# A decoder layer in split fp32 on one core: another order of the same instructions on all engines

## The chip, the cores and the metric

The kernel runs on one core of a Trainium2 chip. The core has a matmul engine (TensorE, PE in the profile; PEld is its loading of weights), three engines for elementwise work (VectorE or DVE, ScalarE or ACT, GpSimd or POOL) and SyncE (SP), from whose queue most DMA transfers are issued; some are issued from POOL's queue. Each engine works through its own queue strictly in order; semaphores hold an instruction until what it reads is written and what it overwrites has been read. The metric is the device time of one execution in microseconds (us); lower is better.

## The reference

One post-norm decoder layer over 512 tokens of width 1024, all in float32. What is computed, cut to its lines:

```python
h = x @ w_in[l]
y_a = nsa_attention(nsa_q, cmp_k, cmp_v, slc_k, slc_v, win_k, win_v, nsa_gate, ...) @ w_nsa_out[l]
y_b = gated_deltanet(gdn_qkv, gdn_beta, gdn_decay, gdn_gate, ...) @ w_gdn_out[l]
mix = (jax.nn.sigmoid(gate_a) * y_a + jax.nn.sigmoid(gate_b) * y_b) @ w_o[l]
x = layer_norm(DEEPNORM_ALPHA * x + mix, ln1_g[l], ln1_b[l])
f = conv_ffn(x, ffn_w_up[l], ffn_conv_w[l], ffn_w_down[l])
x = layer_norm(DEEPNORM_ALPHA * x + f, ln2_g[l], ln2_b[l])
```

The attention (8 heads of 64, 2 key groups) has three branches: keys compressed in blocks of 32, selected blocks of 64, and a window; each is a softmax with distance penalties, and the branches are added with sigmoid gates. The gated DeltaNet (4 heads of 128) passes q, k and v through a causal convolution of 4 taps and silu, solves a triangular system in each chunk of 64 tokens, and carries a state from chunk to chunk. The feed-forward part has a width of 2816, with a causal convolution of 3 taps behind the up-projection and a gated product.

## The kernel before

Every large matrix product is done in three passes so that it keeps float32 accuracy. An operand is split into a high part (rounded to the fast matmul type fp32r) and the residue, and `product` adds three matmuls per 128 rows of the contraction:

```python
PE.matmul(ps, wh[k], mh_(k), ...)   # L532, high x high
PE.matmul(ps, wh[k], ml_(k), ...)   # L534, high x residue of the activations
PE.matmul(ps, wl[k], mh_(k), ...)   # L535, residue of the weights x high
```

A weight tile comes by DMA into `raw` (L511, on SP's queue, 512 KB, three buffers). `split_w` then makes, for each half, `wh` by a cast (L518 on ACT, or L520 on DVE or POOL) and `wl` by a subtraction (L522, on DVE or POOL), three buffers each. The products of the input projection collect in PSUM tiles called gps (two banks in turn), so a new product can begin only when the one before the last has been read out.

The first 460 us or so interleave, on all engines, the input projection with what hangs on it. The names that the change and the prediction speak of are these.

- `conv_silu` makes the convolution of q, k and v: acc (L681 on ACT, then L689 on DVE, or a tap by L686 on ACT and L687 on POOL), then th (L692, ACT) and the result (L699 on DVE: vraw for v). `trans4` transposes vraw on PE (L703, into dps).
- `queries` reads one gps three times: q on ACT (L962) and DVE (L963), then qf on ACT (L964). `keys` does the same for kh (L948, ACT) and kl (L950, DVE).
- `scores` makes scores with two matmuls (L1079, L1080, into aps), a masked maximum on DVE (L1083), exponentials on ACT (L1085), and a scaling by one over the sum (L1087, then L1094 on ACT or L1096 on DVE). `flip` transposes them on PE (L1112), splits them (L1115, L1116), and multiplies by the values (L1126, L1132). At a head's end ob (L1134, ACT) and oT (L1138, DVE) take the result out.
- `gdn_inv` solves the triangular system by steps of tmp and xs on DVE (L815, L816) and small matmuls (L831 to L871).
- `merge` gates the two mixers' projections (mt, L1158 on ACT, L1236 and L1238 on DVE).
- `sums` and `sums_o` (L561, L551) are DMA transfers on POOL's queue between DRAM regions. They form sums of weight blocks, wsum (2816 KB each) and osum (1024 KB each), that later stages load as weights in place of some products.

From about 460 us on, the feed-forward part runs: up-projection (pu), convolution and gate, then the down-projection (px, pz). The last normalization ends the program.

The order of the work isn't left to the order in which the code is written. At the end, `queues(tc)` takes the instructions of each engine as they were made, numbered from 0, and strings them into the order that the table QUEUES names; TURNS then interleaves the five queues into one sequence:

```python
chain(rows[k])                      # one engine's instructions in the order of QUEUES
chain([next(names[x]) for x, n in re.findall(r"([A-Z])(\d*)", TURNS) for _ in range(int(n or 1))])
```

In TURNS "DP4A" means the next instruction of DVE, four of PE, one of ACT (G is POOL, S is SP). The semaphores are placed for that sequence, and buffers change hands along it.

Of the kernel before, what the change touches and what calls it, by code (L numbers as in the profile page):

```python
# [71 lines left out]
def layout(a):  # L72
# [60 lines left out]
    "PE": """0-9 14 11-12 17 10 13 15 18 16 19-20 23 29-30 26 24 21-22 31 27 25 32 41 35 28 38 42-43 39 33 36 40 50 53 37 34 54 47  # L133
44 51-52 55 45 62 65 48-49 59 63 46 64 60 56 61 74 66 75 71 76 57 72 67 86 58 77 68-69 73 87 70 83 78-80 88 84 89 85
95-96 90 81 107 82 108 92-93 98 109-110 94 111 91 112 99 113 97 100 114 101-103 115-148 155-178 149-152 104-105 153
106 154 183-205 207 206 208-230 179-182 235-249 259 250 260-263 251 264-267 252 268 231-233 302 253-255 303 256 269
257-258 234 304-307 270-282 308 310-311 309 360-363 283-292 364-367 293-298 368 312 369-371 313 372 388-389 314 373
315 374-378 390-391 379 392-393 380-381 394-396 382 397 383 398-399 299-301 400-406 444-447 407-410 416-418 411
419-422 448-449 423-437 456-457 438-439 458 316 450 317-318 320-321 319 322 451 323 459-461 324-327 462-467 328-339
468-470 340-347 471 513-514 472 348 352 349 353 350-351 354-355 473-474 515 356-359 384-387 452 475-476 501-502  # L140
412-414 477-479 516-517 453-455 415 518-520 503 521-524 504 525-526 440-443 527-528 723 529-530 724-726 531-532 727
480-481 484 482-483 533-534 728 505 729-731 507 732 485 535 733 508 536 486-487 509-510 734-736 506 488-489 737-738
541 490 739-740 542 491-492 751-755 511 543-544 493-494 546 741-742 495 545 496 512 743 497 756-757 744 758 547
498-499 759-760 500 548-551 560-561 745-746 761-763 562 764 565-566 552 765 553 766 537-539 563-564 591 554 592 555
# [12 lines left out]
893 897 894 898-899 895 1071 1024 1203 1205-1208 900-903 1209 1204 1113-1115 1210 1219-1220 904 908-915 905-907
1211-1212 1116 1213-1214 1117 1221 1223 1215 916-923 1216 1118 1224 924-931 1222 1119-1121 1217 1225 932-935 1122-1124
960 1226 1125-1126 1227-1228 961-962 1233 1127 1218 1128-1129 963 1130 1234 1131 964-965 1132-1134 966-967 1141-1142
1135-1136 1235 968 1238 1143-1146 969-970 1147-1148 1239 1149 971 1150-1152 1240 972-973 1241 1252 1153-1154 974-975  # L160
1155-1156 1242 1236-1237 976 1243 1179 1157 1180 1158 1181 1253 1182-1185 1159 1244 1160-1164 1186 1025 1254 1187
1257-1258 1255 1137-1138 1256 1259 1139 1260 1140 1188-1194 1245 1026-1027 1261 1028 1262 1246-1247 1283 1195-1199
1248 1273 1200 1284 1201 1249 1202 1285 1274 1165-1168 1286 1250 1307 1169-1170 1308-1313 1275 1171-1173 1276 1174
1314-1315 1277 1316 1278 1175 1251 1287 1317 1176 1279 1177-1178 1263 1403-1404 1318 1264 1319 1265-1266 1280-1281
1405 1282 1406 1408 1267 1407 1409 1268 1288 1269 1289 1320-1321 1270 1322-1324 1271 1325-1326 1272 1327 1410-1412
1229 1328-1330 1422 1230-1231 1413 1290-1292 1423 1293 1232 1294-1296 1424 1414 1425-1426 1297 1427-1428 1298-1300
1379 1301 1380 1415 1302-1303 1381 1416-1418 1304 1419 1305 1382-1383 1429-1430 1306 1431 1384 1432 1443 1385 1444
1420 1445 1386-1388 1477 1447 1421 1433 1331 1446 1448 1389-1390 1434 1391 1435 1478-1479 1436 1449 1392 1437-1438
# [168 lines left out]
TURNS = """DS2PSPSPSPDSDPSPASPADPSDP2SP4SP4ASP2AD2P2ASP4APDP5DASP4APDP4DASP3APDP4DP2AP4APDP5DAP4AP3DP3DP5AP3APDP4APDP3DPDP4DSP7S  # L337
# [47 lines left out]
def queues(tc):  # L385
# [1233 lines left out]
```

## Time and profile before

| | |
|---|---|
| median of 3 runs | 817.49 us (816.06 to 818.82) |
| profiled execution: its own time | 816.13 us |
| profiled execution: span | 814.3 us |
| mean granted TensorE clock | 0.997 |
| instructions in the profile | 11,754 |
| HBM traffic | 116.72 MB read, 33.55 MB written, 185 GB/s over the span |

A row of a timeline reads: start in us, duration in us, engine, line of the kernel, operation, output<-inputs by the program's names, partitions x elements, how often in a row, and in brackets how long the engine had been idle before and which instruction ended that idle time. A row of the stages reads: the stretch and its length, then the busy us (and the number of instructions) of PE, PEld, DVE, ACT and POOL, then the granted PE clock, the busy share of the DMA engines and GB/s. Matmuls overlap in the records: a 512-wide one is listed with 0.39 us, though the next starts 0.23 us later, so a hole in PE's work is seen in the distance between starts.

### The profile page before, as it was taken

To read this page: it belongs to the slowest core of one execution; us is meant where nothing else is said; L and a number is where in the kernel's file an instruction comes from. 1 tells how busy PE (TensorE), PEld (TensorE's weight loads), DVE (VectorE), ACT (ScalarE), POOL (GpSimd) and SP (SyncE) were. 2 spreads that over 40 slices of the span, in tenths; PEclk is the share of its full clock that TensorE was granted. 3 is DMA by queue.
4 is the path that set the end of the run, shared out by engine and by line. 5 is a ranking of instruction groups with operands and counts; after the bars stand their busy time and mean duration, and the time that the engine had idled before them with its cause. 6 is when DMAs were issued, how large, how long until landed. Compare 5 with 4: busy or idle time off the path is not lost.

```text
span 814.3 us, 11754 instructions
## 1 busy us (share of the span) xinstructions
PE 800.0 (98%) x4144; PEld 670.2 (82%) x4144; DVE 595.8 (73%) x1314; ACT 409.1 (50%) x911; POOL 177.3 (22%) x172
## 2 busy tenths in 40 slices
PE   9999999999999999999999999999999999999995
PEld 8778778788888888888788898888888888888884
DVE  5667589979768964658669956576666766886997
ACT  4453578775577764413254334443443444565641
POOL 0333635042265111052200101122112011000002
PEclk9999999999999999999999999999999999999998
DMA  7326470035416912635357303698763923466763
GB/s 284 107 78 218 132 182 27 27 104 195 82 52 141 206 52 66 168 104 157 102 196 243 130 27 103 150 260 214 200 212 104 237 92 108 143 202 180 249 212 130
DMA packets 43115, 119.58 MB, mean 147 GB/s; under 512 B 3248, under 2 KB 4016, under 8 KB 42800
## 3 DMA queue, kind: packets, MB, share of 16 engines
q1 hardware_dynamic: 31280, 87.37, 33.2%
q0 software_dynamic: 11776, 31.46, 17.0%
q8 instruction: 33, 0.54, 0.3%
q14 instruction: 26, 0.21, 0.1%
HBM read 116.72 MB, written 33.55 MB: 185 GB/s over the span
## 4 chain that ended last, share of the span: by engine, by line
PE 93%; DVE 3%; ACT 1%; DMA 1%; issue 1%; SPq 0%; DVEq 0%; ACTq 0%
PE pu L532 10%; PE pu L535 10%; PE pu L534 10%; PE gps L532 8%; PE gps L535 8%; PE gps L534 8%; PE px L1488 7%; PE pz L1488 4%; PE pw L1324 3%; PE pout L1126 2%; PE aps L1112 2%; PE pu L1324 2%; PE pu L1488 2%; PE pm L532 2%; PE pm L534 2%; PE pm L535 2%
## 5 line engine op out<-in xcount | busy, mean ns | idle before, releaser
L522 DVE TENSOR_TENSOR wl<-raw,wh 128x512 fp32r<-128x512 f32 x146 | 103.9, 717 | 78.6 <-PE pu L535 34.3
L518 ACT ACTIVATE wh<-raw 128x512 fp32r<-128x512 f32 x126 | 78.9, 629 | 138.9 <-PE pu L534 94.8
L532 PE MATMUL pu<-mh,wh 128*128 128x512 f32 (+1 forms) x384 | 131.5, 373 | 0.0
L534 PE MATMUL pu<-ml,wh 128*128 128x512 f32 (+1 forms) x384 | 131.2, 373 | 0.0
L535 PE MATMUL pu<-mh,wl 128*128 128x512 f32 (+1 forms) x384 | 129.5, 373 | 0.0
L532 PE MATMUL gps<-xh,wh 128*128 128x512 f32 x320 | 124.8, 401 | 1.8 <-issue 0.9
L535 PE MATMUL gps<-xh,wl 128*128 128x512 f32 x320 | 126.4, 402 | 0.0
L534 PE MATMUL gps<-xl,wh 128*128 128x512 f32 x320 | 124.2, 399 | 0.0
L535 PEld LDWEIGHTS pu<-mh,wl 128*128 128x128 f32 x384 | 71.3, 188 | 13.1
L534 PEld LDWEIGHTS pu<-ml,wh 128*128 128x128 f32 x384 | 71.5, 188 | 12.6
L532 PEld LDWEIGHTS pu<-mh,wh 128*128 128x128 f32 x384 | 71.0, 188 | 12.7 <-ACT mh L1303 0.2
L1446 DVE SCALAR_TENSOR_TENSOR fa<-pu,fcw,fa 128x511 f32<-128x511 f32 (+1 forms) x88 | 64.7, 744 | 14.0 <-ACT fa L1443 13.4
L1452 POOL TENSOR_TENSOR fth<-fth,fa 128x512 f32<-128x512 f32 x22 | 30.3, 1382 | 199.8 <-DVE fth L1451 141.3
L532 PEld LDWEIGHTS gps<-xh,wh 128*128 128x128 f32 x320 | 60.1, 189 | 13.5 <-issue 2.6
L535 PEld LDWEIGHTS gps<-xh,wl 128*128 128x128 f32 x320 | 60.1, 189 | 10.5 <-DVE wl L522 0.2
L534 PEld LDWEIGHTS gps<-xl,wh 128*128 128x128 f32 x320 | 60.0, 188 | 10.5
L1423 ACT ACTIVATE wh<-raw 128x512 fp32r<-128x512 f32 x67 | 40.5, 627 | 37.9 <-PE px L1488 11.0
L1424 DVE TENSOR_TENSOR wl<-raw,wh 128x512 fp32r<-128x512 f32 x67 | 45.0, 694 | 14.2 <-ACT wh L1423 13.7
L522 POOL TENSOR_TENSOR wl<-raw,wh 128x512 fp32r<-128x512 f32 x30 | 39.9, 1337 | 13.9 <-ACT wh L518 7.0
L573 POOL TENSOR_TENSOR rs<-rs,minus_half 128x1 f32<-128x1 f32 x8 | 9.4, 1175 | 154.0 <-DVE rs L1282 154.0
L1085 ACT ACTIVATE sc<-sc,mn 128x384 f32<-128x384 f32 (+2 forms) x64 | 35.7, 559 | 11.9 <-DVE mn L1083 11.9
L1443 ACT ACTIVATE fa<-pu,fcw 128x512 f32<-128x512 f32 x44 | 29.8, 680 | 20.4 <-PE pu L535 18.8
(362 smaller groups left out, 1698.7 us busy)
## 6 DMA issues: line engine op xcount, KB each, us to landing
raw<-in_up SPq DMA_DIRECT2D x44, 512.0 KB, 4.2
raw<-in_wT SPq DMA_DIRECT2D x40, 512.0 KB, 3.6
wsum<-in_down POOLq DMA_DIRECT2D x6, 2816.0 KB, 21.6
raw<-wsum SPq DMA_DIRECT2D x20, 512.0 KB, 3.8
raw<-in_down SPq DMA_DIRECT2D x15, 512.0 KB, 4.0
osum<-in_wo POOLq DMA_DIRECT2D x6, 1024.0 KB, 10.0
wsum<-wsum POOLq DMA_DIRECT2D x2, 2816.0 KB, 15.6
raw<-in_wm SPq DMA_DIRECT2D x8, 512.0 KB, 3.6
```

Source lines behind the costliest of these rows:

```text
L518: A.activation(wh, r, AF.Copy)
L522: eng.tensor_tensor(wl, r, wh.bitcast(F32), op=OP.subtract)
L532: i = PE.matmul(ps, wh[k], mh_(k), start=(k == 0), stop=False)
L534: PE.matmul(ps, wh[k], ml_(k), start=False, stop=False)
L535: PE.matmul(ps, wl[k], mh_(k), start=False, stop=(k == n - 1))
L1085: A.activation(s[:, i, :n], s[:, i, :n], AF.Exp, scale=-1.0, bias=mn[:, 0, i:i + 1], accum_out=mn[:, 1, i:i + 1])
L1324: PE.matmul(ps[t], a[x](j)[:, ts], w[y][:, j % 2, :], start=fresh and j == 0 and i == 0, stop=j == TT - 1 and i == 2, skip_group_check=True)
L1423: A.activation(hi, raw[:, i], AF.Copy)
L1424: V.tensor_tensor(lo, raw[:, i], hi.bitcast(F32), op=OP.subtract)
L1446: V.scalar_tensor_tensor(acc[:, n:], ps[:, :S - n], w[:, i:i + 1], acc[:, n:], op0=OP.mult, op1=OP.add)
L1452: G.tensor_tensor(th, th, g[1], op=OP.mult)
L1488: m = PE.matmul(ps, a[x][:, j, ts], w[y], start=first and i == 0, stop=last and i == 2, skip_group_check=True)
```

## The change

Only the tables QUEUES and TURNS differ. Every engine executes the same instructions on the same tiles; some stand at other places in its queue. PE has 2,946 of its 3,886 places changed (by 2.9 places in the mean and 45 at most), DVE 886 of 1,250 (3.2, 57), ACT 510 of 798 (2.4, 19), POOL 113 of 168 (5.0, 40), SP 23 of 179 (1.9, 7). The first and the last few instructions of the program stay. Of some hundred changed lines, one pair reads:

```diff
-    "SP": """1 0 2-9 14 10 15 11 16 19 13 17-18 12 20-69 71 75-76 73-74 72 77-78 70 79-128 130-157 129 158-159 161 163 165 167-175
+    "SP": """1-2 0 3-9 14-15 12 11 10 13 16-69 71-72 75-76 74 73 77-79 70 80-128 130-156 129 157-159 161 163 165 167-172 162
```

Three places, in the order of the queues (engine operation output<-inputs, partitions x elements; the number behind a name tells one tile from another).

First, DVE near 107 us, where vraw_1158 is made, which PE then transposes. Before:

```order
L1096 TENSOR_SCALAR sc_1278<-sc_1278,mn_1279,gsig_109 128x128
L721 TENSOR_SCALAR ss0_991<-ss0_991 128x4
L520 CAST wh_1853<-raw_1847 128x512
L1083 ISA sc_1290,mn_1291<-aps_1289,cst_309 128x256
L1083 ISA mn_1291 128x1
L1096 TENSOR_SCALAR sc_1278<-sc_1278,mn_1279,gsig_109 128x128
L1083 ISA sc_1290,mn_1291<-aps_1289,cst_309 128x256
L1083 ISA mn_1291 128x1
L699 SCALAR_TENSOR_TENSOR vraw_1158<-th_1199,acc_1194 128x512
L736 SCALAR_TENSOR_TENSOR gk_1000<-rn_998,bn_325 128x4
L1087 RECIPROCAL mn_1291<-mn_1291 128x2
L734 RECIPROCAL gk_1000<-ss0_991 128x4
```

Now:

```order
L522 TENSOR_TENSOR wl_1851<-raw_1847,wh_1849 128x512
L1083 ISA sc_1290,mn_1291<-aps_1289,cst_309 128x256
L1083 ISA mn_1291 128x1
L721 TENSOR_SCALAR ss0_991<-ss0_991 128x4
L1087 RECIPROCAL mn_1279<-mn_1279 128x2
L520 CAST wh_1853<-raw_1847 128x512
L1096 TENSOR_SCALAR sc_1278<-sc_1278,mn_1279,gsig_109 128x128
L699 SCALAR_TENSOR_TENSOR vraw_1158<-th_1199,acc_1194 128x512
L736 SCALAR_TENSOR_TENSOR gk_1000<-rn_998,bn_325 128x4
L1087 RECIPROCAL mn_1291<-mn_1291 128x2
L721 TENSOR_SCALAR ss1_1059<-ss1_1059 128x4
```

The second L1096 of sc_1278 has gone behind vraw_1158 and gk_1000. The two L1083 of sc_1290 stand earlier, the first of them ahead of the weight residue wl_1851. On PE, at the same place, an L535 of gps_1857 now stands ahead of the transposes of vraw_1158.

Second, DVE near 155 us, where the scores sc_1790 are scaled (L1096), which PE then transposes. Before:

```order
L816 TENSOR_TENSOR xs_1683<-xs_1683,tmp_1685 128x4x8
L1138 TENSOR_TENSOR oT_1471<-pout_1568,ob_1622 64x512
L1083 ISA sc_1805,mn_1806<-aps_1804,cst_309 128x384
L1083 ISA mn_1806 128x1
L815 TENSOR_TENSOR tmp_1685<-lx_1666,xs_1683 128x4x7
L1087 RECIPROCAL mn_1791<-mn_1791 128x1
L816 TENSOR_TENSOR xs_1683<-xs_1683,tmp_1685 128x4x7
L1096 TENSOR_SCALAR sc_1790<-sc_1790,mn_1791,gsig_109 128x512
L815 TENSOR_TENSOR tmp_1685<-lx_1666,xs_1683 128x4x6
L1087 RECIPROCAL mn_1806<-mn_1806 128x1
```

Now:

```order
L1083 ISA sc_1805,mn_1806<-aps_1804,cst_309 128x384
L1083 ISA mn_1806 128x1
L815 TENSOR_TENSOR tmp_1685<-lx_1666,xs_1683 128x4x7
L1087 RECIPROCAL mn_1791<-mn_1791 128x1
L816 TENSOR_TENSOR xs_1683<-xs_1683,tmp_1685 128x4x7
L815 TENSOR_TENSOR tmp_1685<-lx_1666,xs_1683 128x4x6
L1096 TENSOR_SCALAR sc_1790<-sc_1790,mn_1791,gsig_109 128x512
L816 TENSOR_TENSOR xs_1683<-xs_1683,tmp_1685 128x4x6
L1087 RECIPROCAL mn_1806<-mn_1806 128x1
```

The addition oT_1471 stood ahead of the scaling; it now stands 13 instructions behind it, and one tmp_1685 of the triangular solver has moved ahead.

Third, the beginning of POOL's queue, some 30 us into the program. Before:

```order
L520 CAST wh_542<-raw_540 128x512
L522 ISA
L522 TENSOR_TENSOR wl_544<-raw_540,wh_542 128x512
L520 CAST wh_546<-raw_540 128x512
L522 TENSOR_TENSOR wl_548<-raw_540,wh_546 128x512
L687 TENSOR_TENSOR acc_507<-acc_507,tap_510 128x510
L520 CAST wh_586<-raw_584 128x512
L687 TENSOR_TENSOR acc_507<-acc_507,tap_513 128x509
L763 TENSOR_TENSOR grh_782<-cst_309,gdh_327 128x512
L520 CAST wh_590<-raw_584 128x512
```

Now:

```order
L520 CAST wh_542<-raw_540 128x512
L561 DMA wsum1_101<-in_down 1408x1x512
L522 ISA
L522 TENSOR_TENSOR wl_544<-raw_540,wh_542 128x512
L551 DMA osum1_105<-in_wo 512x1x512
L1063 MEMSET pth_332 128x2x128
L520 CAST wh_546<-raw_540 128x512
L520 CAST wh_586<-raw_584 128x512
L522 TENSOR_TENSOR wl_548<-raw_540,wh_546 128x512
L687 TENSOR_TENSOR acc_507<-acc_507,tap_510 128x510
L520 CAST wh_590<-raw_584 128x512
```

The large copy wsum1 stood at place 27 and is now the second thing that POOL does; osum1 and a MEMSET come soon behind it. The casts wh_586 and wh_590 stand further ahead among the sums acc_507.

Elsewhere: on ACT, qf_417 near 28 us stands ahead of the cast wh_478 instead of behind it; on DVE, x_896 near 94 us stands ahead of the sum acc_1102 (L689) instead of behind it, and bn_325 and one sacc_360 no longer ahead of q2_422 near 27 us; on PE, an L535 of gps_550 near 42.5 us stands ahead of the first L532 of gps_594, which needs the bank that kl_462 reads; on ACT near 167 us, an L1094 of sc_2183 stands ahead of x_1774 and ym_1781 instead of behind them. From 460 us on, some DVE subtractions wl (L522, L1424) stand behind one or two other DVE operations that they preceded.

More of the change, by code (lines that the diff above doesn't have):

```diff
@@ new lines @@
+1780 1775 1781 1776 1782-1784 1777 1785 1802 1786-1788 1803-1805 1789-1790 1814 1791 1806-1807 1815 1808 1816
+1809-1811 1817 1792 1818 1812-1813 1819-1820 1793 1821 1826 1822-1823 1794-1795 1824 1827 1825 1828-1829 1796
+1830-1831 1797-1800 1832-1833 1801 1834-1838 1850 1839-1841 1851-1852 1842 1853-1854 1843-1844 1855-1859 1845
+1860-1863 1846-1847 1874 1864 1875 1848 1876 1865-1866 1849 1877-1878 1886-1887 1879 1888 1880 1889 1867-1868 1881
+1890-1891 1882 1869 1883-1884 1892-1893 1885 1894 1870-1871 1895 1898-1900 1896 1901-1903 1897 1904-1908 1872-1873
@@ new lines @@
+3865-3866 3874 3867-3872 3881-3882 3873 3875-3876 3883 3877-3879 3884-3885""",
+    "DVE": """0-2 4 3 5-12 14 13 15-17 49-50 18 80 51 21 20 52 55 22 19 29 56 30 57 81 31 24 32 105 33 25 34-35 53 36-37 58 54 63
+38-44 94 45 92 46 64-65 59-60 73 61-62 74 71 28 47 72 82-83 75-77 84-85 66 78 67 48 70 141 26 143 142 68 144 97 99 101
+153 102-103 98 100 86-87 104 154-155 88-89 156 23 90 106-110 27 111 79 112-115 91 270 116-117 93 118-121 145-147
+122-123 69 124-128 95 129-130 157 131-132 148 133 158 134-135 159 136 162-163 137 164 138-139 161 140 165-166 96
@@ new lines @@
+1159 1176-1177 1162 1180 1165 1179 1183 1182 1140 1139 1184 1172 1185 1173 1186-1187 1192 1175 1197 1181 1178 1198
+1190 1201 1188 1202 1207-1208 1141 1189 1193 1211-1212 1191 1194 1199 1195 1203 1213-1214 1220 1204 1200 1221-1222
+1215 1209 1217 1216 1223 1219 1224 1210 1225-1228 1205 1196 1229-1230 1218 1206 1231-1235 1237 1236 1238-1240 1242
+1241 1243-1246 1248 1247 1249""",
+    "Activation": """1 0 3 2 4-5 7 6 9 8 10-13 15 14 22 19 16 25 20 23 21 26 30 27 17 24 18 28-29 32 40 33-35 41-44 36-39 45 50-52 60 46 53
@@ new lines @@
+659 665 658 669-670 652 636 672 663 667 673 677 666 660 678 671 680 674 681 675 685-686 679 688 676 668 689 693 682
+687 694 696 683 697 701 684 691 695 690 702 704-705 698 692 706 712 710-711 699 713-714 703 715 700 717 716 718
+707-708 719-720 722-723 709 726 725 728 730-731 729 732-733 721 734 727 736-737 739 724 740 742-745 738 746-747 735
+748 751 750 753 756-757 754 758 752 741 759-761 755 762 749 764-765 767-768 771 770 772 766 773 763 774-776 769
+777-797""",
+    "Pool": """8 137 9 101 1 10 12 11 3 13 0 4-6 14-16 18-21 7 103 25-26 31 22 24 2 34 33 100 32 27 37 104 28-29 35 30 41 38 17 23 42
@@ L382 @@
+P3S2P2DP3AP4DAP3DP3DSPAP3AP3DP2DP4DPAP2SPDP2AP3DPAP2AD2SP4APDP2APDP3DPAPDPSP2DP2AP3DAP3ADSP3DASP4APDP3DP3DP5DPAP3SDPA
+P2DPAP2DP2DPAP2DPSP2D2P3SPAPDP3DAPDP2DP2APDSP2DPDGPAP2DP3D2PAP2DP2DPSP2D2PSAGP2APSDP2DP3DPSP2D2P2AP2AP2DPAP2D2AP4DP3DS
+P2APDSPAPDP3DP3DP2DP3ADP2APDP3DP3DPDP3SP2DP4DP3DPD2PGP3DP3DP3DP5SDP4SP2DSD6GD3S2"""
 PINS = """"""
```

466 lines of the change are left out of this document (221 added, 245 removed).

## The prediction

> **What bounds the kernel now.** I read the busy times and the chain first, then the busy time by stage, then the matmul engine's (PE's) own waits.
>
> ```profile
> PE 800.0 (98%) x4144; PEld 670.2 (82%) x4144; DVE 595.8 (73%) x1314; ACT 409.1 (50%) x911; POOL 177.3 (22%) x172
> PE 93%; DVE 3%; ACT 1%; DMA 1%; issue 1%; SPq 0%; DVEq 0%; ACTq 0%
> ```
> ```profile
> 0.00:6.00 6.00, 4.09 (x20) 3.90 (x21) 2.01 (x5) 2.01 (x3) 0.19 (x4) 1.00 0.68 187
> 6.00:60.00 54.00, 52.74 (x277) 44.67 (x276) 35.02 (x84) 27.66 (x71) 14.98 (x16) 1.00 0.46 156
> 60.00:460.00 400.00, 397.06 (x2233) 331.88 (x2232) 303.66 (x808) 223.17 (x577) 117.45 (x120) 1.00 0.45 130
> 460.00:698.00 238.00, 238.00 (x1141) 200.38 (x1140) 158.00 (x263) 97.79 (x168) 36.20 (x27) 1.00 0.56 151
> 698.00:806.00 108.00, 108.00 (x483) 89.42 (x481) 92.63 (x148) 58.43 (x94) 7.57 (x5) 1.00 0.61 187
> 806.00:814.30 8.30, 0.09 (x1) 0.00 (x0) 4.48 (x10) 0.00 (x0) 0.92 (x1) 0.75 0.60 232
> ```
>
> PE is busy 98% of the span and carries 93% of the chain, at a granted clock of 1.00 in every stage up to the last matmul. A new order changes neither the number of matmuls nor the length of one; it can only remove time in which PE has nothing ready. From 460 to 806 us PE is never idle, and the last 8.3 us hold the closing normalization, whose order is unchanged. So the whole prize lies before 460: 6.00 - 4.09 = 1.91 us at the start, 54.00 - 52.74 = 1.26 up to 60, 400.00 - 397.06 = 2.94 up to 460, in all 6.1 us or 0.75% of the span. The list of PE's waits (engine, line, what it waited for; total, count, longest) says where:
>
> ```profile
> PE gps L605 <- DVE vm L602: 1.4, 1, 1.4
> PE dps L703 <- DVE vraw L699: 1.0, 1, 1.0
> PE aps L1112 <- DVE tmp L815: 0.9, 1, 0.9
> PE gps L532 <- issue: 0.9, 1, 0.9
> PE gps L532 <- ACT mt L1158: 0.5, 1, 0.5
> PE pb L587 <- ACT xh L498: 0.5, 1, 0.5
> PE gps L532 <- DVE kl L950: 0.2, 1, 0.2
> ```
>
> The 1.4 and one 0.5 (pb) belong to the first 5 us, to data that has not arrived; the change leaves that alone. What remains is four single waits near 1 us and some of 0.2 to 0.3.
>
> **The change, wait by wait.** For each I compare the row that releases PE with what now stands ahead of it, and PE's own queue likewise. A wait shrinks when the releasing work loses something ahead of it, or when PE gets other matmuls ahead of the waiting one.
>
> The transposes of vraw, near 109 us:
>
> ```profile
> 106.61 0.35 DVE L1096 TENSOR_SCALAR sc<-sc,mn,gsig 128x128 f32<-128x128 f32 x1
> 108.22 0.69 DVE L699 SCALAR_TENSOR_TENSOR vraw<-th,acc 128x512 f32<-128x512 f32 x1
> 109.05 0.41 PE L703 MATMUL dps<-ident,vraw 128*128 128x128 f32 x2 [1.01 <-DVE vraw L699]
> ```
>
> On DVE one L1096 now stands behind vraw instead of ahead: it occupied 106.61 to the next start at 106.87, 0.26 us. PE does one 512-wide product more first (L535 of gps_1857). Such matmuls start 0.23 us apart (27.86 and 28.09 in the rows for qf below). Sum 0.26 + 0.23 = 0.49 of the 1.01. The sums acc (L689) get one L1083 put ahead of them, so a small wait can appear just before; it costs nothing more, since PE then reaches vraw that much later.
>
> The transposes of the scores sc_1790, near 155.6 us (the view names tmp L815, which no transpose reads; the data come from the L1096 that ends at 155.51):
>
> ```profile
> 153.44 0.69 DVE L1138 TENSOR_TENSOR oT<-pout,ob 64x512 f32<-64x512 f32 x1
> 154.97 0.54 DVE L1096 TENSOR_SCALAR sc<-sc,mn,gsig 128x512 f32<-128x512 f32 x1
> 155.43 0.19 DVE L815 TENSOR_TENSOR tmp<-lx,xs 128x24 f32<-128x24 f32 x1
> 155.66 0.30 PE L1112 MATMUL aps<-ident,sc 128*128 128x128 f32 x1 [0.95 <-DVE tmp L815]
> ```
>
> The oT addition (0.69) moves behind it, one tmp (0.19) ahead: sc is ready 0.50 sooner. On PE the matmuls ahead shrink by one, 0.23, since others now stand behind the transpose. Net gain 0.50 - 0.23 = 0.27; bounds 0 (if DVE, without oT, waits for the scores instead) and the whole 0.95.
>
> The wait for kl (0.2): PE now does one more product (0.23) before the one that needs the bank. It goes, 0.2. The wait for qf at 28 us, too short for the list, shows in the starts:
>
> ```profile
> 27.86 0.39 PE L534 MATMUL gps<-xl,wh 128*128 128x512 f32 x1
> 28.09 0.39 PE L535 MATMUL gps<-xh,wl 128*128 128x512 f32 x1
> 28.59 0.50 PE L532 MATMUL gps<-xh,wh 128*128 128x512 f32 x1
> 26.89 0.17 DVE L645 TENSOR_SCALAR bn<-tb 128x16 f32<-128x16 f32 x1
> 27.95 0.59 ACT L964 ACTIVATE qf<-gps 64x512 f32<-64x512 f32 x1 [0.31 <-DVE q L963]
> ```
>
> 28.59 comes 0.27 later than the pace. ACT now does qf ahead of a weight cast, but that alone is worth nothing: ACT stood idle 0.31 for the q that DVE makes (L963). On DVE bn (0.17) and one small sacc leave the place ahead of that q: 0.2 gained; bounds 0 and 0.27. At 94 us DVE makes the x copy now ahead of an accumulation instead of behind:
>
> ```profile
> 92.99 0.73 DVE L689 SCALAR_TENSOR_TENSOR acc<-gps,tiny,acc 128x510 f32<-128x510 f32 x1
> 93.69 0.40 PE L535 MATMUL gps<-xh,wl 128*128 128x512 f32 x1
> 94.19 0.55 PE L855 MATMUL dps<-ym,x 32*32 32x32 f32 x16
> ```
>
> Here 0.50 - 0.23 = 0.27 goes. At the other two large waits nothing that sets them has moved: the taps (L686) that free a bank near 37 us ("issue", 0.9) and the mt at 395 us (0.5) stay.
>
> **Sum:** 0.49 + 0.27 + 0.2 + 0.2 + 0.27 = 1.43 us off.
>
> **What could be added.** The place that looks worst in the order is on ACT, where an L1094 moves ahead of ym.
>
> ```profile
> 167.87 0.38 ACT L868 ACTIVATE ym<-dps 64x256 f32<-64x256 f32 x1 [0.51 <-PE aps L1112]
> 168.15 0.39 ACT L1094 ACTIVATE sc<-sc,mn 128x128 f32<-128x128 f32 x1
> ```
>
> Its 0.39 fits into the 0.51 that ACT stood idle there, so nothing; without that idle time it costs 0.39. On POOL the 2.8 MB copy wsum1 and the 1 MB osum1 are issued 20 and more places earlier, among the first weight casts, while SP loads the first weight tiles.
>
> ```profile
> wsum<-in_down POOLq DMA_DIRECT2D x1, 2816.0 KB, 13.2
> raw<-in_wT SPq DMA_DIRECT2D x3, 512.0 KB, 5.5
> raw<-in_wT SPq DMA_DIRECT2D x4, 512.0 KB, 3.6
> ```
>
> Beside it (70 to 95 us) a weight tile landed in 5.5 us, without it (55 to 70) in 3.6: up to 1.9 us later. The cover is the time that a tile lies loaded before its cast (raw has three buffers, and none of PE's waits listed names a DMA), so I cost it at nothing; without that cover the first late tile costs 1.9 us.
>
> From 460 us on, some residues wl move behind one or two other DVE operations. DVE is free there for 238.00 - 158.00 = 80 us and PE never waited, so nothing; where the residue is the last thing ready, it costs the operation put ahead, about the residue's own 0.72. SP's 23 places change by 7 at most, between loads that follow each other; I cost them at nothing for the same cover as the weight tiles.
>
> The large unknown is how long a moved DVE operation takes beside POOL:
>
> ```profile
> 102.65 1.05 POOL L763 TENSOR_TENSOR grh<-cst,gdh 128x512 fp32r<-128x512 f32 x1
> 102.73 1.25 DVE L520 CAST wh<-raw 128x512 fp32r<-128x512 f32 x1
> 106.94 0.42 DVE L520 CAST wh<-raw 128x512 fp32r<-128x512 f32 x1
> 39.65 1.62 DVE L522 TENSOR_TENSOR wl<-raw,wh 128x512 fp32r<-128x512 f32 x1
> L522 DVE TENSOR_TENSOR wl<-raw,wh 128x512 fp32r<-128x512 f32 x146 | 103.9, 717 | 78.6 <-PE pu L535 34.3
> ```
>
> The same cast took 0.42 alone and 1.25 under a POOL operation, the residue wl 1.62 instead of 0.72 in the mean, so 0.8 and 0.9 more. Which operations meet changes with 113 of POOL's 168 places and 886 of DVE's 1,250, to either sign: bounds -0.9 and +0.9 per meeting on PE's path. I take zero in the mean, because the mean of 717 ns over 146 says that most of them meet nothing.
>
> The Trainium skill (SBUF — State Buffer, "Who interferes with whom") has a rule that speaks against the change: DVE and GpSimd share a port pair under an exclusive lock, and "Issue order, not op shape, decides who blocks." By it, durations measured in the old order need not hold in the new one; the pair of casts above agrees. Taken as what decides, it leads to rival C; the sum goes by the rows.
>
> **Rivals.** *A, forecast:* the median of the runs shown is 817.49, the profiled one took 816.13 (span 814.3), 1.4 below. I put the gain on the median: 817.5 - 1.4 = 816.1; own range 814.6 to 817.4 (all five gains plus 1.5 of lucky meetings; none). *B, most waits go:* the rest of vraw (0.5) and sc (0.7), issue (0.9) and mt (0.5) vanish too, because many small moves let DVE and ACT run earlier than a wait-by-wait count sees: 1.4 + 2.6 = 4.0, so 813.5. For it: 2,946 of PE's places moved, so that independent products can fill holes. Against: the releasers of issue and mt stand where they stood. *C, slower:* between 60 and 460 us POOL's 120 operations now meet DVE's at places where PE waits next. Each costs 0.8 to 0.9 and each gain above stays; five such, 5 x 0.9 - 1.4 = +3.1, give 820.6. It decides from two meetings (1.7 over 1.4) and is measurable from five. For it: the stretched rows above. Against: by the list PE waited for DVE only three times between 6 and 806 us (1.0 + 0.9 + 0.2), though such meetings happened. *D, the order doesn't do what it says:* each wait removed reappears at the next producer, since DVE's and ACT's work is the same in sum: 817.5.
>
> **How the numbers follow.** A 0.45, B 0.28, C 0.16, D 0.11. Measurable here is about 0.3%, 2.45 us: below 815.0 or above 819.9. Faster: B 0.28 and the low fifth of A, 0.09, 0.37. Slower: C and 0.01 of D, 0.17. Same: 0.46. The range goes from 812.3 (B with all of the 1.26 + 2.94 idle and 1 us at the start gone) to 820.3 (C at nearly its price).
>
> **What would show it.** In the new profile's waits of PE: vraw near 0.5, the L1112 wait near 0.7, kl gone, issue (after the taps) near 0.9 and mt near 0.5 unchanged; PE's idle time 6 to 460 us near 2.8; no idle behind 460; the tail 8.2 us. A weight tile landing late near 35 us as PE's wait would break the claim on the early copy; a residue wl or cast of over 1.2 us just ahead of a PE wait would speak for C; PE's idle time below 1.5 for B.

## The result: faster by 0.6%, and the profile after

The changed kernel takes 812.37 us (median of 4 runs, 812.08 to 812.98), the kernel before 816.98 beside it (4 runs, 816.06 to 818.82). The ratio is 0.9937, with a 95% interval of 0.9923 to 0.9951. That is 4.6 us off, and the interval lies below 1; the prediction had no measurable change, 816.1. The profiled execution of the changed kernel took 812.98 (span 811.2), 3.15 less than the profiled one of before. The busy times and the chain, from the page of the changed kernel:

```profile
PE 800.3 (99%) x4144; PEld 670.8 (83%) x4144; DVE 592.9 (73%) x1314; ACT 409.7 (51%) x911; POOL 175.4 (22%) x172
PE 92%; DVE 4%; DMA 2%; ACT 1%; issue 0%; DVEq 0%; ACTq 0%
```

PE's work is the same to 0.3 us; only its gaps shrank. Its waits (engine, line, what it waited for; total, count, longest):

```profile
PE gps L605 <- DVE vm L602: 1.4, 1, 1.4
PE gps L532 <- ACT tap L686: 1.1, 1, 1.1
PE px L1488 <- DVE x L1525: 0.4, 1, 0.4
PE aps L1079 <- DVE mn L1083: 0.2, 1, 0.2
```

Of the seven waits of before, five are gone: vraw, the scores, mt, xh and kl. The wait for the taps, listed before under "issue", stays. By stage (stretch and length, then busy us of PE, PEld, DVE, ACT, POOL, granted clock, DMA share, GB/s):

```profile
0.00:6.00 6.00, 4.56 (x20) 4.41 (x21) 1.92 (x5) 2.12 (x3) 0.19 (x4) 1.00 0.68 193
6.00:60.00 54.00, 52.92 (x278) 45.53 (x279) 34.39 (x85) 28.16 (x72) 16.32 (x17) 1.00 0.66 228
60.00:460.00 400.00, 399.76 (x2261) 335.41 (x2260) 305.79 (x816) 225.21 (x578) 117.39 (x120) 1.00 0.42 122
460.00:698.00 238.00, 238.00 (x1126) 199.59 (x1125) 156.69 (x260) 98.43 (x170) 33.63 (x26) 1.00 0.56 151
```

PE's idle time from 6 to 460 us falls from 4.20 to 1.08 + 0.24 = 1.32. The transposes of vraw now find their data (timeline, rows of DVE and PE):

```profile
104.97 0.68 DVE L699 SCALAR_TENSOR_TENSOR vraw<-th,acc 128x512 f32<-128x512 f32 x1
106.17 0.39 PE L534 MATMUL gps<-xl,wh 128*128 128x512 f32 x1
106.40 0.27 PE L703 MATMUL dps<-ident,vraw 128*128 128x128 f32 x1
```

vraw is ready at 105.65, and PE comes to it at 106.40, 0.23 after the matmul ahead: no hole, and 0.75 us of room. So it is with the first transpose of sc_1790:

```profile
151.07 0.53 DVE L1096 TENSOR_SCALAR sc<-sc,mn,gsig 128x512 f32<-128x512 f32 x1
151.69 0.40 PE L534 MATMUL gps<-xl,wh 128*128 128x512 f32 x1
151.92 0.27 PE L1112 MATMUL aps<-ident,sc 128*128 128x128 f32 x1
```

The scores end at 151.60, 0.3 ahead of PE. At mt the hole is smaller, but there:

```profile
391.87 0.39 PE L535 MATMUL gps<-xh,wl 128*128 128x512 f32 x1
392.34 0.47 PE L532 MATMUL gps<-xh,wh 128*128 128x512 f32 x1
```

0.47 - 0.23 = 0.24 is left of 0.71 (before: 395.11 to 396.04, less the pace). And one hole is new, just ahead of the scores:

```profile
148.84 0.27 PE L1112 MATMUL aps<-ident,sc 128*128 128x128 f32 x1
149.27 0.44 PE L1079 MATMUL aps<-kh,q 128*128 128x384 f32 x1 [0.16 <-DVE mn L1083]
```

At 151.92 the next matmul starts 0.03 behind the same kind of transpose; here it takes 0.43, so 0.40 is lost. Read in this way, from start to start less the pace (0.23 for most, 0.32 for a 512-wide matmul behind a narrow one, as at 36 us), the larger holes of before and after are these (us):

| place (time before) | before | after | predicted gain |
|---|---|---|---|
| 8.5, first products | 0.28 | 0 | none named |
| 28, qf | 0.27 | 0 | 0.2 |
| 36, taps | 1.02 | 1.24 | 0 |
| 42, kl | 0.33 | 0 | 0.2 |
| 94, x | 0.28 | 0 | 0.27 |
| 105 and 108, acc and vraw | 1.45 | 0 | 0.49 |
| 149 after, mn | 0 | 0.40 | none named |
| 154, scores | 1.11 | 0 | 0.27 |
| 168, ym | 0.30 | 0 | 0 |
| 213, kh | 0.25 | 0 | none named |
| 395, mt | 0.71 | 0.24 | 0 |

The differences sum to 4.1 us; holes that stay below 0.25 in both aren't in the table. By the starts of the same matmuls in both traces, PE leads by 0.8 at 60 us, 3.0 at 115, 3.3 from 155 to 385 and 4.0 at 460. The lead is still 3.9 at 740, and falls to 2.6 at 790 in this one execution.

### The profile page after: what moved, and what is told of

Read it like the earlier page. It is cut to its first block, busy times and chain, and to the rows that moved or that the text cites. A ratio compares the mean times of both kernels' runs of the same rounds, so it can differ in the third digit from the quotient of the medians.

```text
span 811.2 us, 11750 instructions
## 1 busy us (share of the span) xinstructions
PE 800.3 (99%) x4144; PEld 670.8 (83%) x4144; DVE 592.9 (73%) x1314; ACT 409.7 (51%) x911; POOL 175.4 (22%) x172
## 4 chain that ended last, share of the span: by engine, by line
PE 92%; DVE 4%; DMA 2%; ACT 1%; issue 0%; DVEq 0%; ACTq 0%
PE pu L532 10%; PE pu L535 10%; PE pu L534 10%; PE gps L532 9%; PE gps L535 9%; PE gps L534 9%; PE px L1488 4%; PE pw L1324 3%; PE pout L1126 2%; PE aps L1112 2%; PE pu L1324 2%; PE pz L1488 2%; PE pu L1488 2%; PE pm L532 2%; PE pm L535 2%; PE pm L534 2%
## 5 line engine op out<-in xcount | busy, mean ns | idle before, releaser
L522 DVE TENSOR_TENSOR wl<-raw,wh 128x512 fp32r<-128x512 f32 x146 | 103.0, 709 | 79.8 <-ACT wh L518 35.1
L535 PE MATMUL pu<-mh,wl 128*128 128x512 f32 (+1 forms) x384 | 131.2, 372 | 0.0
L532 PE MATMUL pu<-mh,wh 128*128 128x512 f32 (+1 forms) x384 | 129.6, 374 | 0.0
L532 PE MATMUL gps<-xh,wh 128*128 128x512 f32 x320 | 124.3, 400 | 1.2 <-ACT tap L686 1.1
L535 PE MATMUL gps<-xh,wl 128*128 128x512 f32 x320 | 124.8, 399 | 0.0
L535 PEld LDWEIGHTS pu<-mh,wl 128*128 128x128 f32 x384 | 71.4, 188 | 13.0
L532 PEld LDWEIGHTS pu<-mh,wh 128*128 128x128 f32 x384 | 71.0, 188 | 12.7 <-ACT wh L518 0.2
L532 PEld LDWEIGHTS gps<-xh,wh 128*128 128x128 f32 x320 | 59.9, 188 | 12.7 <-POOL wh L520 1.4
L535 PEld LDWEIGHTS gps<-xh,wl 128*128 128x128 f32 x320 | 60.0, 188 | 10.5
L1424 DVE TENSOR_TENSOR wl<-raw,wh 128x512 fp32r<-128x512 f32 x67 | 45.4, 704 | 16.3 <-ACT wh L1423 14.8
L522 POOL TENSOR_TENSOR wl<-raw,wh 128x512 fp32r<-128x512 f32 x30 | 40.6, 1358 | 16.1 <-PE gps L535 7.9
```

Source lines behind the costliest of these rows:

```text
L522: eng.tensor_tensor(wl, r, wh.bitcast(F32), op=OP.subtract)
L532: i = PE.matmul(ps, wh[k], mh_(k), start=(k == 0), stop=False)
L535: PE.matmul(ps, wl[k], mh_(k), start=False, stop=(k == n - 1))
L1424: V.tensor_tensor(lo, raw[:, i], hi.bitcast(F32), op=OP.subtract)
```

## The experiments

All are built from the two orders; the instructions are always the same. Where a table takes fewer lines, line numbers lie up to a few lower than in before (L700 for L703). "Rest" is DVE, ACT, POOL and SP. Ratios are to runs of the kernel before on the same chip, whose median was 816.4 to 816.9.

### Where the gain lies: before 460 us

At 462.5 us both sequences have executed the same set of instructions, so they can be cut and joined there. One kernel takes the new order up to that point, the other behind it.

```diff
 # sequence of all engines: new order first, old behind (the second kernel: the other way round)
-old[:3888] + old[3888:]
+new[:3888] + old[3888:]
```

> The new order up to 462.5 us, the old order behind it (the two tables hold exactly the same instructions up to there). Theory 1, the gain is made by waits before 460 us: PE's lead at 460 us is 4.0 us in the two profiles, so 817.0 - 4.0 = 813.0 or less. Theory 2, the new order behind 460 us costs what its profile shows there (the lead falls from 4.0 at 740 us to 2.65 at 800): then this kernel is about 1 us faster than the whole change, 811.4. Rival, a sizeable part of the gain is made behind 460 us: 814.5 or more.

> The old order up to 462.5 us, the new order behind it. Theory 1: as before, 817.0. Theory 2 (the late order costs): 818.0. Rival (part of the gain is made behind 460 us): 815 or less.

The new order up to 462.5 gives 812.15 (5 runs; ratio 0.9944, 0.9931 to 0.9958), the whole gain. The new order behind it gives 816.46 (11 runs; 1.0002, 0.9994 to 1.0011): nothing. The 1.3 us that the trace of the changed kernel loses from 745 to 790 us needn't be the late order's doing: the trace of the new order behind 462.5 loses nothing there, and that of the first kernel, with the old order there, loses 0.4 near 715 us. Of the 1.3, 0.5 is a hole at 787 us, where PE waits for x (0.4 in the list above); what causes the rest, and why it differs between traces, wasn't found.

### How much comes by 115 us

```diff
-old[:957] + old[957:]
+new[:957] + (the rest, in the old order)
```

> The new order up to about 115 us, the old one behind it. By the lead of the two profiles, 3.0 us at 110 to 130 us, the time should be 817.0 - 3.0 = 814.0, with the old waits at 154, 168, 213 and 395 us still there (1.1 + 0.3 + 0.25 + 0.7). By the prediction's sum only 0.49 + 0.2 + 0.2 + 0.27 = 1.2 comes from this part: 815.8.

814.05 (6 runs; 0.9967, 0.9956 to 0.9978): 2.5 us of the 4.4, where the prediction's terms for this part (vraw, kl, qf and x) sum to 1.2. Its waits, from the list:

```profile
PE gps L531 <- ACT tap L685: 1.1, 1, 1.1
PE aps L1111 <- DVE tmp L814: 0.9, 1, 0.9
PE pm L531 <- ACT wh L517: 0.6, 1, 0.6
PE gps L531 <- ACT mt L1157: 0.5, 1, 0.5
```

vraw is gone, and so are kl, qf and x by the starts; the taps, the scores and mt stand as before. The order behind 115 us removes the last two. The wait in pm is new: at 369 us PE needs a weight cast, and the cast waits for its weight tile:

```profile
368.37 0.63 ACT L517 ACTIVATE wh<-raw 128x512 fp32r<-128x512 f32 x1 [3.88 <-DMA raw<-in_wm]
```

Here PE's lead, 2.4 us from 115 us on, falls to 1.7. Neither before nor the whole change has this wait. So what an order gains early can be lost in part at a later producer.

### The vraw wait: one cast, the rest, PE, and all

My sum had taken one L1096 off DVE's way to vraw. The order also puts a weight cast ahead of the sums acc, at a time when DVE is idle. That move alone:

```diff
 L1050 TENSOR_TENSOR cs_1134<-cs_1134,csm_1143 128x512
+L520 CAST wh_1849<-raw_1847 128x512
 L689 SCALAR_TENSOR_TENSOR acc_1194<-gps_1169,tiny_310,acc_1194 128x511
-L520 CAST wh_1849<-raw_1847 128x512
```

> The old order with one move: DVE's cast wh_1849 (L520), which took 1.25 us at 102.73, stands ahead of the first sum acc_1194 (L689) instead of behind it, so that it runs in the 4.14 us in which DVE was idle there. Theory: this one move is most of what the prediction missed at 109 us; the waits for acc at 105 (0.28) and vraw at 109 (1.17) shrink by 1.2 together: 815.8. Rival (the chain to vraw is set elsewhere, by th or by PE's products): both waits stay, 817.0.

816.0 (11 runs; 0.9989, 0.998 to 0.9998). The timeline, rows of DVE and PE:

```profile
100.86 1.40 DVE L520 CAST wh<-raw 128x512 fp32r<-128x512 f32 x1 [3.20 <-PE gps L534]
107.28 0.69 DVE L699 SCALAR_TENSOR_TENSOR vraw<-th,acc 128x512 f32<-128x512 f32 x1
108.11 0.41 PE L703 MATMUL dps<-ident,vraw 128*128 128x128 f32 x2 [0.70 <-DVE vraw L699]
```

The cast now stands in DVE's idle time (3.20 us of it are left ahead of the cast); PE leads by 0.70 behind it, more than the 0.49 that I gave the place. The other way round, the whole change with this cast put back:

```diff
-L520 CAST wh_1849<-raw_1847 128x512
 L1083 ISA sc_1278,mn_1279<-aps_1277,cst_309 128x128
 L1083 ISA mn_1279 128x1
 L689 SCALAR_TENSOR_TENSOR acc_1194<-gps_1169,tiny_310,acc_1194 128x511
+L520 CAST wh_1849<-raw_1847 128x512
```

> The whole change with one move undone: the cast wh_1849 stands behind the first sum acc_1194 again. If the cast is what freed vraw, a wait of 0.7 to 1.2 comes back before the transposes of vraw or before gps_1857 and the time is 813.1 to 813.6; if the rest of the new order carries it, nothing comes back and the time is 812.4.

812.43 (4 runs), the time of the change. vraw starts at 106.03 instead of 104.97, and still no wait for it is listed: the new order reaches the place with room, so no single move carries it.

Then the stretch from 96 to 113 us alone: PE's new order, the rest's, and both.

```diff
 # 96 to 113 us: the first kernel, the second, the third
-PE old, rest old
+PE new, rest old
+PE old, rest new
+PE new, rest new
```

> Only PE, only between 96 and 113 us, has the new order; the rest as before. Theory J (only both orders together): the two waits here (0.28 for acc, 1.17 for vraw by the starts) don't shrink in sum by more than 0.3, and new ones may come. Theory B (room on PE): PE has some 0.7 us more products ahead of the transposes of vraw, so 0.7 goes. The prediction's count: 0.23.

> Only between 96 and 113 us, DVE, ACT, POOL and SP have the new order, PE the old one. Prediction's count: 0.26 less. Theory J: as much or less, perhaps with new waits for products that PE makes late. If DVE's cast and the order of the sums carry it: 1.0 or more less.

> Only between 96 and 113 us, all engines have the new order. Theory J: both waits gone, 1.4 below before. Prediction's count: 0.49.

815.57, 815.52 and 814.85 (10 runs each; ratios 0.9991, 0.9987 and 0.9981, each with 0.0010 or less either way). PE alone, rows of DVE and PE:

```profile
109.66 0.69 DVE L699 SCALAR_TENSOR_TENSOR vraw<-th,acc 128x512 f32<-128x512 f32 x1
110.50 0.30 PE L703 MATMUL dps<-ident,vraw 128*128 128x128 f32 x1 [0.53 <-DVE vraw L699]
```

The rest alone:

```profile
106.16 0.68 DVE L699 SCALAR_TENSOR_TENSOR vraw<-th,acc 128x512 f32<-128x512 f32 x1
107.03 0.38 PE L703 MATMUL dps<-ident,vraw 128*128 128x128 f32 x2
```

Across this stretch PE gains 1.0 us by its own order, 1.6 by the rest's, and 1.85 by both. By PE's order alone the hole for acc goes and 0.92 - 0.23 = 0.69 is left at vraw, so 0.76 of the 1.45 of both; the other 0.25 comes from small matmuls of the solver that stand closer together. The hole at x, ahead of this stretch, stays in all three. So either part does much of it, and what one has gained the other can't gain again. By the medians the gains are 0.9, 0.9 and 1.6, with about 0.8 us of uncertainty each. In the second and third trace PE then waits at 369 us for the same weight cast as in the kernel with the new order to 115 us, and loses 0.7 of its lead there.

### Engines apart, over 60 to 285 us

Both kernels cut at points that both sequences share in order, PE's new order in one, the rest's in the other.

```diff
 # 60 to 285 us: the first kernel, the second
-PE old, rest old
+PE new, rest old
+PE old, rest new
```

> Between 60 and 285 us PE has the new order, all other engines the old one; the rest as before. The prediction gave PE's own moves 0.23 of gain at vraw and 0.23 of loss at the scores: the time of before. Theory B, that the room lies in how many products stand between what PE makes for a chain and what it takes back (at vraw 37 instead of 33, at the scores 21 instead of 17, about 0.7 and 0.4 us more work): both waits shrink by that, 1.1 us below before, and the holes left are about 0.8 at vraw and 0.7 at the scores.

> Between 60 and 285 us DVE, ACT, POOL and SP have the new order, PE the old one; the rest as before. The prediction gave these engines 0.26 at vraw, 0.50 at the scores and 0.27 at x: 1.0 us below before. Theory B adds the cast wh_1849 at vraw (0.7, as in the run with that move alone) and takes away most of the scores' 0.50, because DVE's maximum L1083 would now wait for PE's products aps_1804: 0.26 + 0.7 + 0.1 + 0.27 = 1.3 below before, with the hole before the transposes of the scores still 1.0 or more.

828.6 (4 runs; 1.0144, 1.0128 to 1.0161) and 832.28 (5 runs; 1.0181, 1.0163 to 1.0199): 12 and 16 us slower. In the whole change PE gains some 2.7 us across the same stretch (its lead goes from 0.8 to about 3.5); both halves together, with the old order around them, weren't run. The prices by which the parts would simply add fell with this. Each half brings waits that neither whole has: for tmp 2.4, sc 1.6 and 1.5, y 1.3 and pcl 1.0 in the first, for sc 2.2, the taps 1.8, ym 1.7, vn 1.3 and mn 1.3 in the second.

### The scores: PE, the rest, and all

The same for 140 to 170 us alone. On PE, around the waiting transpose:

```diff
-L1080 MATMUL aps_1789<-kl_462,q2_576 128x512
-L1112 MATMUL aps_1653<-ident_311,sc_1626 128x128
-L535 MATMUL gps_2261<-xh_93,wl_2255 128x512
-L1112 MATMUL aps_1653<-ident_311,sc_1626 128x128
 L1132 MATMUL pout_1568<-pcl_1155,vm_111 128x512
 L532 MATMUL gps_2261<-xh_93,wh_2257 128x512
+L534 MATMUL gps_2047<-xl_94,wh_2043 128x512
+L1112 MATMUL aps_1814<-ident_311,sc_1790 128x128
```

> Only between 140 and 170 us, and only PE, has the new order. The prediction's count says the wait of 0.95 before the transposes of the scores (1.1 by the starts) grows by 0.23. Theory B: PE has about 0.4 us more products between the scores and their transposes, DVE works as before since oT holds it until 154.13: the wait shrinks by 0.4 to about 0.6 (0.7 by the starts). Neither gives zero.

> Only between 140 and 170 us, DVE, ACT, POOL and SP have the new order, PE the old one. The prediction's count: the scores are ready 0.50 us sooner, the wait falls from 0.95 to 0.45. Theory B: with oT gone from its place DVE's maximum L1083 waits for PE's second matmul of aps_1804, which ends at 154.01, 0.12 before oT ended; one tmp (0.2) has moved ahead of the scaling: the wait stays at 0.9 to 1.1. If both B answers hold, it is the two orders together that take the wait away.

> Only between 140 and 170 us, all engines have the new order; the rest as before. Theory J (the orders pay only together): the wait before the transposes of the scores (1.1 by the starts), which was 2.6 with PE's new order alone and 1.2 with the other engines' alone, is gone, and so is the one for ym (0.3): about 1.2 below before. Sum of the two runs apart (the parts add up): 3.5 + 1.7 above before.

PE alone: 819.94 (7 runs; 1.0036, 1.0024 to 1.0048). The timeline, rows of PE, ACT and DVE:

```profile
154.67 0.40 PE L534 MATMUL gps<-xl,wh 128*128 128x512 f32 x1
157.47 0.30 PE L1112 MATMUL aps<-ident,sc 128*128 128x128 f32 x1 [2.40 <-DVE tmp L815]
154.64 0.59 ACT L1134 ACTIVATE ob<-pout 64x512 f32<-64x512 f32 x1 [2.41 <-PE pout L1132]
155.27 0.68 DVE L1138 TENSOR_TENSOR oT<-pout,ob 64x512 f32<-64x512 f32 x1 [2.21 <-ACT ob L1134]
156.78 0.54 DVE L1096 TENSOR_SCALAR sc<-sc,mn,gsig 128x512 f32<-128x512 f32 x1
```

PE's new order closes a head's output (L1132) later. In the old order of the rest, ob and oT still stand ahead of the exponentials and of sc, so ACT stands still for 2.41 us, DVE for 2.21, and PE in turn for their scores: the hole grows from 1.11 to 2.80 - 0.23 = 2.57.

The rest alone: 818.09 (10 runs; 1.0017, 1.0008 to 1.0026), of its waits:

```profile
PE aps L1112 <- DVE xs L816: 1.1, 1, 1.1
PE aps L1112 <- ACT sc L1094: 1.0, 1, 1.0
```

The wait of the scores isn't shorter, by starts 1.24, although oT has left its place ahead of sc; and a second one appears ahead of it. DVE's row shows why: without oT, its maximum, which stands ahead of the scaling, waits for PE's second matmul of aps_1804.

```profile
155.58 0.56 DVE L1083 CUSTOM_DVE_ANT_0 sc<-aps,cst 128x384 f32<-128x384 f32 x1 [0.65 <-PE aps L1080]
```

This is the lower bound that the prediction named, 0. Without PE's new order, DVE's gain of 0.50 counts for nothing here.

All together: 816.54 (10 runs; 0.9997, 0.9985 to 1.0008). By itself this time tells no gain; in its trace the hole at the scores is gone, and PE, which lost 0.6 just ahead of the place (a hole of 0.4 at mn among it), gains 1.05 across it, 0.45 in sum; this execution had begun 0.8 us late. The parts, added, would be 3.5 + 1.7 = 5.2 us slower. So at this place the two halves need each other.

### mt

PE's new order from 384 to 398 us alone. The last matmul of pm0, which feeds mt, moves ahead of two matmuls of gps_4515: 10 of these, not 8, now stand between it and the matmul that waits for mt.

```diff
-L532 MATMUL gps_4515<-xh_93,wh_4511 128x512
 L535 MATMUL pm0_4552<-yoh_3954,wl_4546 128x512
...
-L534 MATMUL gps_4515<-xl_94,wh_4511 128x512
...
+L532 MATMUL gps_4515<-xh_93,wh_4511 128x512
+L534 MATMUL gps_4515<-xl_94,wh_4511 128x512
+L535 MATMUL pm0_4552<-yoh_3954,wl_4546 128x512
```

> Only PE, only between 384 and 398 us, has the new order: two products of gps_4515 (0.45 us) go behind the last product of pm0 instead of ahead of it. Prediction: the mt wait stays, since its releaser has not moved. Theory B (room between what PE gives and what it takes back): the wait, 0.71 by the starts, falls by 0.45 to about 0.25, and the lead behind 400 us is 0.45.

816.3 (10 runs; 0.9985, 0.9973 to 0.9996). PE's rows:

```profile
387.22 0.39 PE L534 MATMUL pm<-yol,wh 128*128 128x512 f32 x1
387.71 0.50 PE L535 MATMUL pm<-yoh,wl 128*128 128x512 f32 x1
...
395.33 0.39 PE L535 MATMUL gps<-xh,wl 128*128 128x512 f32 x1
395.80 0.47 PE L532 MATMUL gps<-xh,wh 128*128 128x512 f32 x1
```

The hole at mt falls from 0.71 to 0.47 - 0.23 = 0.24, as in the whole change: 0.47 less, about the two products (2 x 0.23). But pm0's residue is now asked for earlier, and 0.26 is lost at 387 (0.11 more behind it). The trace shows 0.1 us gained in sum; the median's 0.56 has an uncertainty of 0.9.

### The early copies

The whole change, with the issue of wsum1 put back to where it was, near 70 us; and the same with osum1 moved there as well.

```diff
 # POOL, first kernel: wsum1 alone; second kernel: osum1 too
-L561 DMA wsum1_101<-in_down 1408x1x512
 L522 TENSOR_TENSOR wl_544<-raw_540,wh_542 128x512
-L551 DMA osum1_105<-in_wo 512x1x512
...
 L806 TENSOR_TENSOR gx_832<-f16_815,cst_309 128x256
+L561 DMA wsum1_101<-in_down 1408x1x512
 L573 TENSOR_TENSOR rn_532<-ss0_525,minus_half_321 128x4
-L551 DMA osum1_105<-in_wo 512x1x512
+L551 DMA osum1_105<-in_wo 512x1x512 x2
```

> The whole change with wsum1 alone issued at its old place (near 70 us), osum1 early as in the change. Prediction: the early transfer of wsum1 is hidden, 812.4 as the whole change. Rival: weight tiles land later beside the transfer near 70 to 84 us and PE waits there, 813.5 or more.

> The whole change, but POOL issues wsum1 and osum1 at their old places (near 70 us) instead of near 32 us. Prediction: the early issue is hidden, 812.4 as the whole change. Rivals: the early transfer costs (the wait of 1.2 near 35 us for the taps, 1.0 before, has its 0.2 from it): 812.2 or less; or it pays, since later weight loads run without it: 813 or more.

wsum1 alone: 811.54 (4 runs, 811.42 to 811.72; 0.9936, 0.992 to 0.9953), the lowest median of all, though against before its ratio is the change's. Its trace lacks most of the change's loss from 745 to 790 us, and PE is some 0.3 ahead of the change's from the first 60 us on. So the early copy gains nothing that can be seen; whether it costs some tenths isn't settled.

With osum1 too: 823.56 (4 runs; 1.0079, 1.0063 to 1.0096). Rows of POOL and PE:

```profile
72.46 0.93 POOL L551 DMA_DIRECT2D osum<-in_wo  x1
86.29 1.22 POOL L551 DMA_DIRECT2D osum<-in_wo  x1 [12.90 <-DMA osum<-in_wo]
86.97 3.06 POOL L522 TENSOR_TENSOR wl<-raw,wh 128x512 fp32r<-128x512 f32 x2
88.85 0.80 PE L535 MATMUL gps<-xh,wl 128*128 128x512 f32 x1 [8.53 <-POOL wl L522]
```

This is my edit's own fault: the second transfer adds to what the first one writes, so it waits 12.90 us on POOL's queue, and two residues wl behind it wait with it. It doesn't tell what the early osum1 is worth by itself. It shows what keeps this wait hidden: the two transfers onto osum1 are issued 26 us apart before (83.5 and 110.0) and 37 apart in the change (34.1 and 71.5).

## Why the prediction was wrong, step by step

Forecast was no measurable change, from a sum of 1.43 us of gains; the change is 4.6 us faster. The steps that failed are the term for vraw (0.49, measured 1.45 with the hole for acc), the term for the scores (0.27, from a count with the wrong sign; the hole of 1.11 went) and mt, put at nothing (0.47 measured). That 812.37 lies inside the stated range, 0.07 above its low end, is no support for the sum: the low end stood for all idle time from 6 to 460 us gone, and 1 us at the start with it; 1.32 us of that idle time is still there.

**What bounds the kernel:** right. PE's gaps before 460 us were the prize, and the gain came from nowhere else (second experiment: nothing behind 460). The sign "no idle behind 460" failed by the one wait for x (0.4).

**The start, "the change leaves that alone":** not settled. The wait for xh (0.5) is gone from the list. PE's first products pb and ACT's casts there do stand in another order, which I hadn't looked at. But this wait varies: it is listed with 0.3 to 0.9 in eleven of the twelve traces with the old start, with 1.1 and 0.2 in two of the six with the new one, and not at all in the other four.

**vraw, "0.26 + 0.23 = 0.49":** mis-sized. It is 1.17, and the 0.28 ahead of it too. The failing step on DVE is that I counted one L1096. The rest's order alone brings 1.6 us; its cast, put into DVE's idle time, brings 0.70 by itself, though the whole order doesn't need it. Which other moves make up the 1.6 wasn't tried apart. PE's part was 0.76, not 0.23: I had counted one more product ahead of vraw from the program's start on. Between the last product of gps_1169, which feeds acc, and the first transpose of vraw stood 32 matmuls, and 36 stand there now. The four more are two of 512 columns, one of 256 and a transpose of 128, about 2 x 0.23 + 0.12 + 0.1 = 0.7 us of work.

**The scores, "the matmuls ahead shrink by one, 0.23":** wrong in sign. This count too was made from the program's start. The count that bears on the wait is that of the matmuls between the product that feeds DVE's chain and the transpose that takes its result: between the L1080 of aps_1804 and the first L1112 into aps_1814 these were 3, and are 11 now. That DVE does wait for this L1080 once oT is away is shown by the run of the rest alone; there the 0.50 on DVE didn't count by itself (still 1.24). Nor does the count on PE by itself, because ob and oT stand in the chain then. All of the 1.11 went, by both together; the new hole at mn ahead of it takes 0.40 back.

**kl, qf and x (0.2, 0.2, 0.27):** right in kind and nearly in size; the holes of 0.33, 0.27 and 0.28 are gone with the order up to 115 us. Which move took each away wasn't tried apart.

**"Nothing that sets them has moved: the taps and mt stay":** right for the taps (1.02 to 1.24), wrong for mt. ACT's and DVE's side of mt stood, but PE's own order had moved: 10 matmuls instead of 8 behind the last one of pm0, 2 x 0.23 = 0.46, and the hole lost 0.47. PE's new order alone does this.

**Edits costed at nothing:** no cost of the early wsum1 or of the late residues wl stands clear of the noise (812.37 with them, 811.54 with wsum1 put back, 812.15 with the old order behind 460 us). SP's places weren't tried alone. ym, covered at 168 us by 0.51 of idle, even lost its hole of 0.30.

**DVE beside POOL, zero in the mean:** no loss from it was found. The stretch itself is real: the cast of wh_1849 took 1.25 before, 0.77 after, 1.40 in the experiment that moved it alone, each time beside POOL operations. Durations did depend on who met whom. The Trainium skill's rule on this (SBUF — State Buffer, "Who interferes with whom") agrees with these three rows; it didn't decide the time.

**Rivals.** C is out: in the list of waits none is for a wl or a cast. D is out for the whole change, whose gain stays up to 740 us, but not in kind: the hole of 0.40 at mn is such a wait, and so is the one at 369 us in three kernels with part of the order. B had the time within 1.1 us (813.5) and its mark, idle time below 1.5 (it is 1.32); of its four waits three went and the taps stayed, which the scores' and vraw's full holes made up for. My argument against it, that the releasers stand where they stood, looked at one side of the wait only. Its argument for, independent products that fill holes, is what the run at mt shows, and, with the other engines' order beside it, those at vraw and the scores.

## What to carry to other kernels

When an order is judged by its differences, follow a loop: the matmul that feeds a chain on other engines, the chain, the matmul that takes the result. Count the independent work between the two ends on the waiting engine, not from the program's start, and judge all engines' moves together: half of this change, over 60 to 285 us, cost 12 or 16 us; the whole saved 4.6. Where only part of an order is tried, an unrelated instruction left ahead of the chain (ob and oT here) can cost more than the place was worth.

## What the runs showed of the hardware

**A wait can cost more than its length.** After the hole of 2.57 us with PE's order alone at the scores, the granted clock fell (by stage, columns as above):

```profile
158.00:159.00 1.00, 1.00 (x4) 0.79 (x3) 0.53 (x3) 0.43 (x1) 0.00 (x0) 0.50 0.00 0
160.00:161.00 1.00, 1.00 (x5) 0.81 (x3) 0.85 (x7) 1.00 (x4) 0.00 (x0) 0.50 0.00 0
```

For about 3.2 us 512-wide matmuls started 0.43 apart instead of 0.23, which adds some 1.55 us to the 1.46 by which the hole had grown: 3.0 of the 3.5 us lost. PE's new order over 60 to 285 us has the same hole at the same place, and the clock stays (timeline of PE, then the stage):

```profile
159.79 0.30 PE L1109 MATMUL aps<-ident,sc 128*128 128x128 f32 x1 [2.41 <-DVE tmp L812]
```
```profile
160.00:161.00 1.00, 1.00 (x6) 0.82 (x6) 0.91 (x5) 0.62 (x1) 0.00 (x0) 1.00 0.00 0
```

So length alone doesn't decide. The rest's new order over 60 to 285 us shows it too: there the clock is at 0.50 behind a shorter wait, whose hole by the starts is 2.12 - 0.23 = 1.89 (92.63 to 94.75; PE, then the stage).

```profile
94.75 1.08 PE L832 MATMUL dps<-ym,x 128*128 128x64 f32 x8 [1.73 <-DVE ym L829]
```
```profile
97.00:98.00 1.00, 1.00 (x4) 0.70 (x4) 0.00 (x0) 0.00 (x0) 1.00 (x2) 0.50 0.70 270
```

PE had been at work again for some 1.7 us when the clock fell there, so that this hole is the cause isn't shown. The three holes of 1.0 to 1.2 us of before left its clock at 1.00; behind the wait of 8.5 us the clock was at 0.50 for some 5 us more. The Trainium skill (TensorE: Matmul & The Clock Gate, "HAM oscillation — how this bites in real kernels") gives as its rule no idle gap above about 3.4 us; here the clock was at 0.50 right behind a gap of 2.57, so as a bound that rule is too wide. The free-running window that the same page of the Trainium skill describes ("What's actually happening") would explain why the same hole acts in one run and not in another; no run here tested that.

**The first microseconds vary by more than most edits.** In the profiled execution of before, the 288-wide matmuls of pb start 0.24 apart at first and 0.13 apart from 5.72 on:

```profile
5.48 0.40 PE L587 MATMUL pb<-wh,xh 128*128 128x288 f32 x1 [0.48 <-ACT xh L498]
5.72 0.29 PE L588 MATMUL pb<-wl,xh 128*128 128x288 f32 x1
5.85 0.42 PE L587 MATMUL pb<-wh,xh 128*128 128x288 f32 x2
```

In that of PE's order alone over 96 to 113 us, where nothing differs yet, they are still 0.25 apart at 6.54 and beyond 8 us:

```profile
6.54 0.44 PE L588 MATMUL pb<-wl,xh 128*128 128x288 f32 x1
6.79 0.68 PE L587 MATMUL pb<-wh,xh 128*128 128x288 f32 x2
```

By 10 us PE is 2.3 us behind, and this execution took 818.41 beside a median of 815.57 for the same kernel. Single executions of this kernel can't be compared at the level of 2 us; the lead of PE, read between two points of the program, can.
